# Second feed-forward layer: shift and scale made block by block at its beginning, 40 tiles of outer products with parts in SBUF

## Chip, cores and metric

One core of one Trainium2 chip runs the whole program. The metric is device time in microseconds (us), the median of three runs. A profile of one further execution comes with it; its trace is what is read here. PE is TensorE, DVE VectorE, ACT ScalarE, SP the engine whose queue issues nearly all DMAs.

## What is computed

A block of three sublayers on x (256 rows, width 2048), each scaled and shifted by numbers that come from a vector c:

```
mod = (silu(c) @ w_ada + b_ada).reshape(1, 3, 3, 2048)        # w_ada: 2048 x 18432
def sublayer(x, fn, pre, post, shift, scale, gate, weight):
    h = rms_norm(x, pre) * (1 + scale) + shift
    return x + weight * (1 + gate) * rms_norm(fn(h), post)
x = sublayer(x, ffn1, ..., mod[0,0], mod[0,1], mod[0,2], 0.5)
x = sublayer(x, mixer, ..., mod[1,0], mod[1,1], mod[1,2], 1.0)
x = sublayer(x, ffn2, ..., mod[2,0], mod[2,1], mod[2,2], 0.5)
# ffn(h) = (silu(h @ w_gate) * (h @ w_up)) @ w_down, inner width 5632
```

The mixer is a recurrent time mix (heads of 64) with a small pooling branch between two matrix products. All weights are float32 in device memory and pass through the chip once, 497.8 MB in all.

## The kernel before

**Products.** Each float32 weight piece is loaded by SP (`load`, L169, tile `raw`), split into a rounded part by ACT (L179, `hi`) and the rest by DVE (L180, `lo`), and multiplied in three terms. `mm3` (L189 to L191) issues three matmuls of 256 columns for one tile of 128 output columns and one of the 16 k-tiles of the input; `mm3_wide` (L196, L197) issues the same three terms as one matmul of 512 columns and one of 256. The input `hT` is held transposed, 16 k-tiles, each as rounded part and rest.

**Feed-forward layers.** `ffn` begins with `outer`: the k-tiles of `hT` come in blocks of 2, 2, 4, 4 and 4 (`FIRST_BLOCKS`, which `BLOCKS` equals), and each block is multiplied, as it becomes ready, into a number of gate and up tiles whose sums stay open. `first` of the 44 inner tiles keep their sums in PSUM; `spill` more have them in SBUF, where ACT copies the first part (L604) and DVE adds each later one (L606); their first two blocks are merged into one of four k-tiles (`MERGE`). The remaining inner tiles use `mm3_wide` over all 16 k-tiles. The inner tiles are taken in groups; after each group its down product is added to `y`. The first layer has `first` 4, `spill` 16 and groups of 20, 16, 8; the second has 6, 0 and groups of 12, 12, 12, 8.

**Next block.** Before a block of the second layer is multiplied, DVE updates x (L517), ACT scales its rows (L338), PE transposes them (L353), and ACT and DVE apply scale and shift (L357, L361, L362) with the columns in `mod`.

**Shift, scale, gate ("ada").** `ada_begin` lays down a list of tasks, `ada_step` takes the next quarter of one. A task is 1024 columns of `w_ada` over all 2048 rows (8 MB): SP loads 512 KB pieces into four (in the mixer two) buffers, DVE multiplies each by a column of silu(c) and adds it to `acc` (L242 the first, L244 the other 15), and at the end the 128 partitions are summed: for one vector by a DVE transpose and reduction (L256, L258) and matmuls L261; for a pair of vectors (shift and scale) by matmuls with ones, L251. The order is (1, 0) by blocks, then 2, 4, 3, 5, 7, 6, 8; vectors 7 and 6 are scale and shift of the second layer, 8 its gate. Steps are spread by counting loads: one per 2.8 loads in the first layer, one per 3 in the mixer, one per 12 in the second layer; in the outer product of the first layer, three per block (`TICKS`). `ada_finish` takes what is still missing at a place that needs it. The first layer gets through vectors 0 to 4 and 6 of the 8 steps of 5; 18 steps are left to the mixer (2 of vector 5, 8 each of 7 and 6), all taken by the end of its second `w_out` pass.

**Order.** A tile framework places the instructions of each engine from priorities; each engine then takes its own in order. `later` (L277) keeps ada work of DVE behind the first block's `hT` where a layer begins.

Of the kernel before, what the change touches and what calls it, by code (L numbers as in the profile page):

```python
# [23 lines left out]
FF_OUTER = 4  # L24
FF_SPILL = 16
MERGE = 4
FIRST_BLOCKS = ((0, 2), (2, 2), (4, 4), (8, 4), (12, 4))
TICKS = (1, 3, 7)
GROUPS1 = (20, 16, 8)
GROUPS2 = (12, 12, 12, 8)  # L30
ADA_FFN1, ADA_MIXER, ADA_OUT, ADA_FFN2 = 2.8, 3, 3, 12
BLOCKS = ((0, 2), (2, 2), (4, 4), (8, 4), (12, 4))
POOL_WIDTH = 512
# [43 lines left out]
class Block:  # L77
# [232 lines left out]
    def row(self):  # L310
        return self.tile(self.small, [P, 1], tag="row", bufs=32)
# [215 lines left out]
    def rows_block(self, load, nkt, per, x, banks, apart, done, more=(), warm=None, wide=1):  # L527
# [33 lines left out]
        for b, part in enumerate(parts):  # L561
# [4 lines left out]
            with self.tc.high_priority() if apart else nullcontext():  # L566
                done(*part, banks[b][:, :part[2]])

    def outer(self, blocks, loads, block, tick, piece):


# [3 lines left out]
        for q, (b0, bn) in enumerate(blocks):  # L575
            block(b0, bn)
            for i, (w, c0, n, outs, parts) in enumerate(loads):
                k0, kn = b0, bn
                if parts is not None and b0 + bn <= MERGE:
                    if b0 + bn < MERGE:  # L580
                        tick(q, i)
                        continue
                    k0, kn = 0, MERGE
                raw = self.load(w, k0, kn, c0, n)
                tick(q, i)
                nk = min(kn, (512 if self.gates else piece) // n)
                row, t0, t1 = outs, 0, KD - 1
                if parts is not None:
                    banks = [outs() for _ in parts]
                    row = [((2 * b + j) * P, bank[:, j, :], j == 0, j == 1) for b, bank in enumerate(banks)  # L590
                           for j in range(2)]
                    t0, t1 = k0, k0 + kn - 1
                for pc in range(0, kn, nk):
                    hi, lo = self.split(raw[:, pc:pc + nk, :])
                    for off, ps, first, last in row:
                        for k in range(nk):
                            kt = k0 + pc + k
                            cs = slice(off, off + P)
                            self.mm3(ps, hi[:, k, cs], lo[:, k, cs], self.hT[:, kt],
                                     first and kt == t0, last and kt == t1)  # L600
                if parts is not None:
                    for part, bank in zip(parts, banks):
                        if k0 == 0:
                            nc.scalar.copy(part, bank)  # L604
                        else:
                            nc.vector.tensor_tensor(part, part, bank, ALU.add)  # L606
# [141 lines left out]

    def tick(self):
        self.chunks += 1  # L750
        if int(self.chunks / self.every) > int((self.chunks - 1) / self.every) and self.ada_pos < self.ada_end[(6,)]:
            self.ada_step(self.mm)

    def mixer(self, ctx):
        nc, tc, I = self.nc, self.tc, self.I
# [37 lines left out]
        def stage(n, extra=None):  # L793
            runs = [extra] if extra else []
            if n - 1 in state:
                runs.insert(0, self.rwkv_m(n - 1, state[n - 1]))
            if n - 2 in state:
                runs.insert(0, self.rwkv_b(n - 2, state[n - 2]))
            while runs:
                runs = [run for run in runs if next(run, self) is not self]  # L800
# [43 lines left out]
        for q, tags in ((0, ("mm", "mm", "sa", "ga")), (2, ("pb", "zb")), (3, ("sb", "y", "mm"))):  # L844
            banks = [row(t) for t in tags]
            if q == 3:
                self.ada_finish((6,), self.mm)
            w = 2 if q == 0 else 1

            def load(kc):  # L850
                raw = self.load(I["w_out"], 4 // w * kc, 4 // w, q * 512, w * 512)
                self.tick()
                return raw

            def done(tt, c0, n, ps):
                self.post_rows(q + c0 // 512, tt, c0 % 512, n, ps)

            place = lambda tags: lambda shape: [self.tile(self.w2p, shape, F32R, tag=t, bufs=3 if t == "ar" else 2) for t in tags]
            more = [place(t) for t in (("SV", "S0"), ("ar", "bk")) * 2]
            self.rows_block(load, KD, 1, lambda k: self.hT[:, k], banks, q == 3, done, more, self.mm, w)  # L860
# [288 lines left out]
    def begin(self, mm):  # L1149

        nc, I = self.nc, self.I
        self.x = self.tile(self.big, [P, 2, D], tag="x")
        self.y = self.tile(self.big, [P, 2, D], tag="y")
        self.yT = self.y.rearrange("p t (k c) -> p (t k) c", c=T)
        self.hT = self.tile(self.big, [P, KD, 2, T], F32R, tag="hT")
        self.col = {}
        vec = lambda *names: [(n, I[n]) for n in names]
        self.csilu = self.tile(self.const, [P, KD], tag="csilu")
        nc.scalar.activation(self.csilu[:, :1], self.eps, AF.Silu)
        self.load_columns(vec("c"), mm)  # L1160
        for a, n, ap in self.columns("c", 0, KD):
            self.use_ln_exp([nc.scalar.activation(self.csilu[:, a:a + n], ap, AF.Silu)])
        self.ada_begin(((1, 0), (2,), (4,), (3,), (5,), (7,), (6,), (8,)))
        for i in range(5):
            if i == 3:
                for tt in range(2):
                    self.load_x(tt)
            if i == 1:
                self.load_columns(vec("norm_pre", "norm_post", "pool_scale", "k_k"), mm)
                self.load_columns([("b_ada", I["b_ada"][:P * P])], mm)  # L1170
            if i < 4:
                self.ada_step(mm)
        for tt in range(2):
            self.pre_begin(tt)
# [27 lines left out]
    def run(self):  # L1202
        I = self.I
        self.constants()
        with ExitStack() as ph:
            mm, actp = self.ffn_pools(ph)
            self.begin(mm)

            def block(k0, n):
                q = [b[0] for b in FIRST_BLOCKS].index(k0)  # L1210
                self.ada_finish(((1, 0), q), mm)
                for tt in range(2):
                    self.pre_rows(tt, k0, n)
                self.pre_block(0, k0, n, mm)

            def tick(q, i):
                if q == len(FIRST_BLOCKS) - 1:
                    if i == 0:
                        self.begin_rest(mm)
                elif i in TICKS:  # L1220
                    self.ada_step(mm)

            self.ffn(I["ffn1_w_gate"], I["ffn1_w_up"], I["ffn1_w_down"], ADA_FFN1, mm, actp, FIRST_BLOCKS, block, tick,
                     FF_OUTER, FF_SPILL, (FF_SPILL + FF_OUTER) // 2 - 8, GROUPS1,
                     lambda *a: (self.ada_finish((3,), mm), self.post_begin(0, 0.5, True, mm, *a)), lambda tt: None, True)
        with ExitStack() as ph:
            self.phase(ph, 2, 0, 2, 300)
            self.mixer(ph)
        with ExitStack() as ph:
            mm, actp = self.ffn_pools(ph)  # L1230

            def block(k0, n):
                self.next_block(2, k0, n, mm)

            self.ffn(I["ffn2_w_gate"], I["ffn2_w_up"], I["ffn2_w_down"], ADA_FFN2, mm, actp, BLOCKS,
                     block, lambda q, i: None, 6, 0, 0, GROUPS2,
                     lambda *a: (self.ada_finish((8,), mm), self.post_begin(2, 0.5, False, mm, *a)),
                     self.store, False)

# [26 lines left out]
```

## Time and profile before

| | us |
|---|---|
| median of three runs (2156.7 to 2158.58) | 2158.49 |
| the profiled execution's own time | 2157.36 |
| its span, first to last instruction | 2155.6 |
| PE busy | 2072.4 (96%) |
| DVE busy | 1621.2 (75%) |
| ACT busy | 1079.1 (50%) |

The span falls into the first layer (to about 805 us), the mixer (to about 1402) and the second layer. Read the share of an engine stage by stage, since the averages cover all three. The end of a pipelined matmul is modelled, so a PE that is shown as busy may still lose some time; how fast PE works is read from the starts of matmuls that follow each other. The mean granted clock was 0.984.

### The profile page before, as it was taken

The numbers are of one execution on the slowest core, as the hardware profiler recorded it, in microseconds if no ns is written. First come the engines' busy times: TensorE is split into PE (matmuls) and PEld (weight loads), VectorE is DVE, ScalarE is ACT, GpSimd is POOL, SyncE is SP. The second block draws the span as 40 slices with busy tenths as digits, with TensorE's granted clock in tenths as the row PEclk, the third lists the DMA queues.
The fourth block names the chain that finished last, engine by engine and source line by source line (L and its number), as shares of the span: only waits on it lengthen the run. The fifth ranks groups of instructions, "written<-read, shape, count | busy, mean of one in ns | idle before, by whom it ended". The sixth has DMA issues, their size and how long they took to land.

```text
span 2155.6 us, 37182 instructions
## 1 busy us (share of the span) xinstructions
PE 2072.4 (96%) x14955; PEld 1802.4 (84%) x14955; DVE 1621.2 (75%) x2523; ACT 1079.1 (50%) x1823; POOL 0.2 (0%) x4
## 2 busy tenths in 40 slices
PE   4999999999999998899999999999999999999998
PEld 3999988888888877888887866799888888888887
DVE  6788898798877778899998877788755555555556
ACT  4534543444433455765656654665434444444453
POOL 0000000000000000000000000000000000000000
PEclk8999999999999999999999979999999999999999
DMA  9999888999888748845644526599755555555553
GB/s 317 359 315 322 289 282 306 323 336 315 304 308 294 277 141 243 258 140 173 192 137 147 182 81 195 169 311 320 254 195 194 180 193 196 187 185 195 194 181 133
DMA packets 316570, 502.31 MB, mean 233 GB/s; under 512 B 12037, under 2 KB 197486, under 8 KB 316142
## 3 DMA queue, kind: packets, MB, share of 16 engines
q1 hardware_dynamic: 314380, 496.32, 68.6%
q10 hardware_dynamic: 2018, 3.62, 0.5%
q8 instruction: 117, 1.92, 0.4%
q14 instruction: 55, 0.45, 0.1%
HBM read 497.77 MB, written 2.12 MB: 232 GB/s over the span
## 4 chain that ended last, share of the span: by engine, by line
PE 83%; DMA 7%; DVE 6%; ACT 3%; issue 2%; SPq 0%; DVEq 0%; ACTq 0%
PE mm L196 21%; PE mm L197 10%; PE mm L191 7%; PE mm L190 7%; PE mm L189 7%; PE mm L523 7%; PE mm L525 7%; PE mm L524 7%; DMA ada<-in_w_ada_dram 5%; DVE lo L180 2%; DVE acc L244 1%; DMA raw<-in_w_in_dram 1%; ACT hi L179 1%; PE sb L1110 1%; PE sb L1145 0%
## 5 line engine op out<-in xcount | busy, mean ns | idle before, releaser
L179 ACT CAST hi<-raw 128x1024 fp32r<-128x1024 f32 (+2 forms) x768 | 694.6, 911 | 780.7 <-PE mm L525 266.9
L180 DVE TENSOR_TENSOR lo<-raw,hi 128x1024 fp32r<-128x1024 f32 (+2 forms) x768 | 796.4, 1048 | 351.6 <-ACT hi L179 348.5
L196 PE MATMUL mm<-hT,hi 128*128 128x512 f32 x1984 | 698.6, 395 | 0.0
L197 PE MATMUL mm<-hT,lo 128*128 128x256 f32 x1984 | 558.3, 281 | 2.4 <-DVE lo L180 2.4
L196 PEld LDWEIGHTS mm<-hT,hi 128*128 128x128 f32 x1984 | 373.8, 188 | 87.9
L244 DVE SCALAR_TENSOR_TENSOR acc<-ada,csilu,acc 128x1024 f32<-128x1024 f32 (+1 forms) x285 | 349.0, 1225 | 96.7 <-DMA ada<-in_w_ada_dram 94.7
L190 PE MATMUL mm<-hT,hi 128*128 128x256 f32 x1376 | 395.0, 288 | 3.4 <-DVE hT L362 3.4
L189 PE MATMUL mm<-hT,hi 128*128 128x256 f32 x1376 | 392.0, 289 | 4.0 <-ACT hT L357 3.8
L191 PE MATMUL mm<-hT,lo 128*128 128x256 f32 x1376 | 393.2, 287 | 0.5 <-DVE lo L180 0.5
L197 PEld LDWEIGHTS mm<-hT,lo 128*128 128x128 f32 x1984 | 372.8, 188 | 3.3 <-DVE lo L180 3.1
L189 PEld LDWEIGHTS mm<-hT,hi 128*128 128x128 f32 x1376 | 260.9, 191 | 10.6 <-ACT hT L357 6.1
L190 PEld LDWEIGHTS mm<-hT,hi 128*128 128x128 f32 x1376 | 261.9, 190 | 9.1 <-DVE hT L362 5.5
L191 PEld LDWEIGHTS mm<-hT,lo 128*128 128x128 f32 x1376 | 261.9, 191 | 4.5 <-DVE lo L180 0.7
L523 PE MATMUL mm<-hi,act 128*128 128x512 f32 (+1 forms) x688 | 264.9, 385 | 0.0
L524 PE MATMUL mm<-lo,act 128*128 128x512 f32 (+1 forms) x688 | 264.5, 384 | 0.0
L525 PE MATMUL mm<-hi,act 128*128 128x512 f32 (+1 forms) x688 | 264.4, 384 | 0.0
L524 PEld LDWEIGHTS mm<-lo,act 128*128 128x128 f32 x688 | 129.3, 188 | 25.9 <-DVE lo L180 0.6
L525 PEld LDWEIGHTS mm<-hi,act 128*128 128x128 f32 x688 | 129.3, 188 | 25.7
L523 PEld LDWEIGHTS mm<-hi,act 128*128 128x128 f32 x688 | 129.3, 188 | 25.6
L641 ACT ACTIVATE silu<-silu 128x512 f32<-128x512 f32 x31 | 19.6, 632 | 58.0 <-DVE silu L640 58.0
L644 ACT CAST act<-silu 128x512 fp32r<-128x512 f32 x31 | 19.2, 618 | 31.1 <-DVE silu L642 31.1
L606 DVE TENSOR_TENSOR act<-act,mm 128x512 f32<-128x512 f32 x48 | 32.2, 681 | 1.8 <-PE mm L191 1.6
(371 smaller groups left out, 1936.2 us busy)
## 6 DMA issues: line engine op xcount, KB each, us to landing
ada<-in_w_ada_dram SPq DMA_DIRECT2D x224, 512.0 KB
raw<-in_ffn_w_down_dram SPq DMA_DIRECT2D x88, 1024.0 KB
raw<-in_ffn_w_gate_dram SPq DMA_DIRECT2D x84, 1024.0 KB
raw<-in_ffn_w_up_dram SPq DMA_DIRECT2D x84, 1024.0 KB
raw<-in_w_in_dram SPq DMA_DIRECT2D x34, 1024.0 KB
ada<-in_w_ada_dram SPq DMA_DIRECT2D x128, 256.0 KB
raw<-in_w_out_dram SPq DMA_DIRECT2D x16, 1024.0 KB
raw<-in_w_in_dram SPq DMA_DIRECT2D x9, 512.0 KB
```

The lines of the kernel that those rows point to most:

```text
L179: a = nc.scalar.copy(hi, raw)
L180: d = nc.vector.tensor_tensor(lo, raw, hi.bitcast(F32), ALU.subtract)
L189: nc.tensor.matmul(ps, hi, x[:, 0, :], start=start, stop=False)
L190: nc.tensor.matmul(ps, hi, x[:, 1, :], start=False, stop=False)
L191: nc.tensor.matmul(ps, lo, x[:, 0, :], start=False, stop=stop)
L196: nc.tensor.matmul(ps.rearrange("p a t -> p (a t)"), hi, x.rearrange("p a t -> p (a t)"), start=start, stop=False)
L197: nc.tensor.matmul(ps[:, 0, :], lo, x[:, 0, :], start=False, stop=stop)
L244: self.later(nc.vector.scalar_tensor_tensor(acc, raw[:, i], ck, acc, ALU.mult, ALU.add))
L523: nc.tensor.matmul(ps, x[:, 0, ts], hi, start=start, stop=False)
L524: nc.tensor.matmul(ps, x[:, 0, ts], lo, start=False, stop=False)
L525: nc.tensor.matmul(ps, x[:, 1, ts], hi, start=False, stop=stop)
L606: nc.vector.tensor_tensor(part, part, bank, ALU.add)
```

## The change

The pair (7, 6) becomes five tasks by blocks, as (1, 0) is: 256, 256, 512, 512 and 512 columns of each vector. The mixer takes the first two (`ADA_AHEAD`); the other three, 24 MB in pieces of two 256 KB transfers, are taken in the second layer's outer product, three steps per block, and what is missing at the block that needs it. The second layer gets `first` 4, `spill` 16 (20 inner tiles, 40 of gate and up) and groups 20, 16, 8.

```diff
-GROUPS1 = (20, 16, 8)
-GROUPS2 = (12, 12, 12, 8)
+GROUPS = (20, 16, 8)
+ADA_AHEAD = 1
...
     def tick(self):
         self.chunks += 1
-        if int(self.chunks / self.every) > int((self.chunks - 1) / self.every) and self.ada_pos < self.ada_end[(6,)]:
+        if int(self.chunks / self.every) > int((self.chunks - 1) / self.every) and self.ada_pos < self.ada_end[(7, 6), ADA_AHEAD]:
...
             if q == 3:
-                self.ada_finish((6,), self.mm)
+                self.ada_finish(((7, 6), ADA_AHEAD), self.mm)
...
-        self.ada_begin(((1, 0), (2,), (4,), (3,), (5,), (7,), (6,), (8,)))
+        self.ada_begin(((1, 0), (2,), (4,), (3,), (5,), (7, 6), (8,)))
...
             def block(k0, n):
+                self.ada_finish(((7, 6), [b[0] for b in FIRST_BLOCKS].index(k0)), mm)
                 self.next_block(2, k0, n, mm)
-            self.ffn(I["ffn2_w_gate"], I["ffn2_w_up"], I["ffn2_w_down"], ADA_FFN2, mm, actp, BLOCKS,
-                     block, lambda q, i: None, 6, 0, 0, GROUPS2,
+            def tick(q, i):
+                if i in TICKS and self.ada_pos < self.ada_end[(7, 6)]:
+                    self.ada_step(mm)
+
+            self.ffn(I["ffn2_w_gate"], I["ffn2_w_up"], I["ffn2_w_down"], ADA_FFN2, mm, actp, FIRST_BLOCKS,
+                     block, tick, FF_OUTER, FF_SPILL, (FF_SPILL + FF_OUTER) // 2 - 8, GROUPS,
```

How this moves instructions is seen at three places. Names are the program's tiles with a running number: `lo` and `hi` the split weights, `x`, `hT` and `work` the next block's rows, `acc` and `ada` the sums and pieces of w_ada.

DVE where the second layer begins, from the last `hT` of its first block on. Before:

```order
L362 TENSOR_TENSOR hT_94<-work_15953,hT_94 128x256
L180 TENSOR_TENSOR lo_16002<-raw_15999,hi_16001 128x512
L180 TENSOR_TENSOR lo_16018<-raw_15999,hi_16017 128x512
L180 TENSOR_TENSOR lo_16036<-raw_16033,hi_16035 128x512
L517 SCALAR_TENSOR_TENSOR x_92<-y_93,row_15800,x_92 128x256
L180 TENSOR_TENSOR lo_16054<-raw_16051,hi_16053 128x512
L517 SCALAR_TENSOR_TENSOR x_92<-y_93,row_15892,x_92 128x256
```

and in the changed kernel:

```order
L362 TENSOR_TENSOR hT_94<-work_15815,hT_94 128x256
L180 TENSOR_TENSOR lo_15881<-raw_15861,hi_15880 128x512
L242 TENSOR_SCALAR acc_15863<-ada_15864,csilu_95 128x1024
L180 TENSOR_TENSOR lo_15897<-raw_15861,hi_15896 128x512
L244 SCALAR_TENSOR_TENSOR acc_15863<-ada_15868,csilu_95,acc_15863 128x1024
L517 SCALAR_TENSOR_TENSOR x_92<-y_93,row_15656,x_92 128x256
L244 SCALAR_TENSOR_TENSOR acc_15863<-ada_15872,csilu_95,acc_15863 128x1024
L517 SCALAR_TENSOR_TENSOR x_92<-y_93,row_15748,x_92 128x256
L244 SCALAR_TENSOR_TENSOR acc_15863<-ada_15876,csilu_95,acc_15863 128x1024
L180 TENSOR_TENSOR lo_15965<-raw_15962,hi_15964 128x1024
L244 SCALAR_TENSOR_TENSOR acc_15863<-ada_15912,csilu_95,acc_15863 128x1024
L362 TENSOR_TENSOR hT_94<-work_15950,hT_94 128x256
```

The products with the pieces of w_ada for the third block now stand between the updates and splits of the second. From the first row here (left out) to the sixteenth product DVE has 32 instructions, the 11 above among them: the 16 products, 2 splits of 512 columns and 4 of 1024, 2 updates of 256 and 6 of 512, and 2 `hT`.

SP's queue at the same place in the changed kernel, from the last load for the first block to the last for the second (before, pieces of w_ada stand there too, but nothing of this block waits for them):

```order
L169 DMA raw_15861<-in_ffn_w_up_dram 128x2x512
L238 DMA ada_15864<-in_w_ada_dram 128x512 x2
L238 DMA ada_15868<-in_w_ada_dram 128x512 x2
L238 DMA ada_15872<-in_w_ada_dram 128x512 x2
L238 DMA ada_15876<-in_w_ada_dram 128x512 x2
L169 DMA raw_15962<-in_ffn_w_gate_dram 128x2x512
L238 DMA ada_15912<-in_w_ada_dram 128x512 x2
L238 DMA ada_15916<-in_w_ada_dram 128x512 x2
L238 DMA ada_15920<-in_w_ada_dram 128x512 x2
L238 DMA ada_15924<-in_w_ada_dram 128x512 x2
L169 DMA raw_15992<-in_ffn_w_up_dram 128x2x512
```

The second block's weights now stand behind eight pieces, of which the last four wait for DVE to give back a buffer.

PE at the end of the second block's products with the four tiles whose sums stay in PSUM. Before (PE is at its products with the first block):

```order
L190 MATMUL mm_15950<-hT_94,hi_16053 128x256
L191 MATMUL mm_15950<-hT_94,lo_16054 128x256
L353 MATMUL mm_16076<-consts_69,y_93 128x128 x4
L353 MATMUL mm_16190<-consts_69,y_93 128x128 x4
L189 MATMUL mm_15945<-hT_94,hi_16089 128x256
```

and in the changed kernel:

```order
L190 MATMUL mm_15804<-hT_94,hi_16021 128x256
L191 MATMUL mm_15804<-hT_94,lo_16022 128x256
L251 MATMUL mm_16010<-ones_71,acc_15863 128x1 x8
L189 MATMUL mm_16051<-hT_94,hi_16053 128x256
L190 MATMUL mm_16051<-hT_94,hi_16053 128x256
```

The sum over partitions of the third block's shift and scale, L251, now stands in PE's row between the first 32 products of the layer (4 tiles of gate and of up, 4 k-tiles) and the 128 merged ones of the tiles with parts in SBUF. Before, no ada matmul stands in the outer product, and 48 products of the first two blocks are followed by those of the third.

## Rows read from the trace of the kernel before

**Rows 1.** Windows of the mixer and second layer: start:end, length, busy us by engine, clock.
```profile
860.00:1270.00 410.00, 391.59 (x4994) 338.53 (x4992) 365.35 (x945) 261.02 (x676) 0.00 (x0) 0.98 0.55 169
1270.00:1330.00 60.00, 54.45 (x427) 36.34 (x428) 42.69 (x101) 24.76 (x68) 0.00 (x0) 0.77 0.47 150
...
1560.00:1700.00 140.00, 140.00 (x733) 120.02 (x733) 75.80 (x79) 61.42 (x72) 0.00 (x0) 1.00 0.58 191
```

**Rows 2.** Chain that ended last, mixer: start, length, last matmul of a head pair.
```profile
961.87 0.86 PE sb L1145 x4
...
1026.57 0.87 PE sb L1145 x4
...
1237.77 0.86 PE sb L1145 x4
```

**Rows 3.** Timeline of PE, end of the mixer: start, length, instruction, [idle before, releaser].
```profile
1299.32 1.22 PE L882 MATMUL sa<-G,pool_w 128*128 128x256 f32 x2 [3.35 <-DVE G L880]
```

**Rows 4.** Timeline of PE, second layer, wide products: the first and the 29th.
```profile
1489.81 0.39 PE L196 MATMUL mm<-hT,hi 128*128 128x512 f32 x1
...
1499.70 0.40 PE L196 MATMUL mm<-hT,hi 128*128 128x512 f32 x1
```

**Rows 5.** Timeline of PE, first layer, outer product: the first and the 16th.
```profile
240.06 0.28 PE L189 MATMUL mm<-hT,hi 128*128 128x256 f32 x1
...
245.36 0.28 PE L189 MATMUL mm<-hT,hi 128*128 128x256 f32 x1
```

**Rows 6.** Instructions on `acc`, 805 to 1330: count, ns least/median/most, start of first and last.
```profile
L244 DVE SCALAR_TENSOR_TENSOR acc<-ada,csilu,acc x68: 1266/1278/1286, 816.9 to 1322.7; 128x1024 f32<-128x1024 f32 x68
```

**Rows 7.** Groups by line and shape, whole span: count, busy us, mean ns.
```profile
L244 DVE SCALAR_TENSOR_TENSOR acc<-ada,csilu,acc 128x512 f32<-128x512 f32 x30 | 22.5, 751 | 2.8 <-DMA ada<-in_w_ada_dram 2.0
```

**Rows 8.** Timeline of DVE where the second layer begins.
```profile
1403.64 0.42 DVE L362 TENSOR_TENSOR hT<-work,hT 128x256 fp32r<-128x256 f32 x1
1403.98 1.89 DVE L180 TENSOR_TENSOR lo<-raw,hi 128x512 fp32r<-128x512 f32 x3
1405.79 0.48 DVE L517 SCALAR_TENSOR_TENSOR x<-y,row,x 128x256 f32<-128x256 f32 x1
...
1413.80 0.74 DVE L517 SCALAR_TENSOR_TENSOR x<-y,row,x 128x512 f32<-128x512 f32 x1
1414.46 0.42 DVE L362 TENSOR_TENSOR hT<-work,hT 128x256 fp32r<-128x256 f32 x1
1414.80 0.74 DVE L517 SCALAR_TENSOR_TENSOR x<-y,row,x 128x512 f32<-128x512 f32 x1
...
1417.80 0.75 DVE L242 TENSOR_SCALAR acc<-ada,csilu 128x1024 f32<-128x1024 f32 x1
...
1427.72 1.28 DVE L244 SCALAR_TENSOR_TENSOR acc<-ada,csilu,acc 128x1024 f32<-128x1024 f32 x1
1428.92 1.22 DVE L180 TENSOR_TENSOR lo<-raw,hi 128x1024 fp32r<-128x1024 f32 x1
1430.05 1.28 DVE L244 SCALAR_TENSOR_TENSOR acc<-ada,csilu,acc 128x1024 f32<-128x1024 f32 x1
```

**Rows 9.** Timeline of SP: the first load issued for the second layer.
```profile
1394.13 0.37 SPq L169 DMA_DIRECT2D raw<-in_ffn_w_gate_dram  x1
```

**Rows 10.** DMA from 40 to 110, first layer: packets, bytes, mean rate.
```profile
DMA packets 13118, 25.05 MB, mean 358 GB/s; under 512 B 915, under 2 KB 925, under 8 KB 13112
```

**Rows 11.** Timeline of PE, outer product of the first layer.
```profile
42.55 1.87 PE L251 MATMUL mm<-ones,acc 128*128 128x1 f32 x8 [6.18 <-DVE acc L244]
...
101.54 1.84 PE L251 MATMUL mm<-ones,acc 128*128 128x1 f32 x16
...
283.87 0.40 PE L523 MATMUL mm<-hi,work 128*128 128x512 f32 x1
```

**Rows 12.** Window after the wait at 42.55; columns as in rows 1.
```profile
43.00:53.00 10.00, 9.12 (x42) 8.42 (x43) 7.73 (x11) 4.43 (x7) 0.00 (x0) 0.52 1.05 391
```

**Rows 13.** Timeline of PE, second layer: the first wide product.
```profile
1480.62 0.40 PE L196 MATMUL mm<-hT,hi 128*128 128x512 f32 x1
```

More of the change, by code (lines that the diff above doesn't have):

```diff
@@ L1223, in run @@
             self.ffn(I["ffn1_w_gate"], I["ffn1_w_up"], I["ffn1_w_down"], ADA_FFN1, mm, actp, FIRST_BLOCKS, block, tick,
-                     FF_OUTER, FF_SPILL, (FF_SPILL + FF_OUTER) // 2 - 8, GROUPS1,
+                     FF_OUTER, FF_SPILL, (FF_SPILL + FF_OUTER) // 2 - 8, GROUPS,
                      lambda *a: (self.ada_finish((3,), mm), self.post_begin(0, 0.5, True, mm, *a)), lambda tt: None, True)
```

## The prediction, made before the changed kernel ran

> **What bounds the kernel now.** I read the busy shares by windows first, then the chain that ended last, then the timelines where stages meet. In the second layer PE has no gap (140 us busy of 140), with DVE at 76 of 140. In the mixer both are nearly full: of 410 us PE is busy 391.6 and DVE 365.4. At the mixer's end, 1270 to 1330, PE is busy 54.5 of 60 at a mean granted clock of 0.77 [rows 1]. So work on DVE or in the DMA queues costs nothing in the second layer once it runs. In the mixer, less work on DVE can help, but only as far as PE is waiting there.
>
> How far, two views tell. In the chain the last matmul of a head pair's stage returns after 64.7 us the first time (961.87 to 1026.57), and in the next three periods after 70.4 on average (211.2 by 3) [rows 2]. One period has the same six loads and the same two ada steps as another, so 64.7 can be reached even with that load on DVE, and three periods lose 17 us to it. And at 1299.32 PE has stood 3.35 us, waiting for a small DVE instruction of the pooling [rows 3].
>
> **The change, part by part.**
>
> *Products.* 14 inner tiles, 28 of gate and up, go from `mm3_wide` to `mm3`: 448 products of one tile with one k-tile. A wide product takes 9.89 us by 28 = 0.353 us from start to start [rows 4], three narrow matmuls 5.30 by 15 = 0.353 [rows 5]. I take nothing for it. The Trainium skill speaks against the change here: "TensorE: Matmul & The Clock Gate", section "Wait — 56ns, not 53.3ns?", states a fixed cost of about 2.5 ns for each matmul at full clock. By that the 448 further matmuls would cost 1.1 us, an estimate; the rows show no such difference, and the measurement decides.
>
> *Sums in SBUF.* 16 copies on ACT and 48 additions on DVE are new, 8 additions to `y` (one group less) go. They lie beside PE's matmuls, as in the first layer, whose same loads I use below, so that their cost is in those rows. If that cover went, PE would wait at the end of the outer product; in the first layer it does not: the first down matmul follows without idle time [rows 11].
>
> *The mixer.* It had 18 ada steps of four products: 72 on DVE, 68 of them L244 at 1.28 us [rows 6]; the other 4 are the L242 that begin a task. It keeps 2 such steps (8 products) and gets 8 of half width: 32 products of 0.75 us [rows 7]. As one instruction starts some 0.08 us before the one ahead of it has ended (1.20 from start to start for 1.28) [rows 8], that is 85 us before and 9.6 + 32 x 0.67 = 31 us now: 54 us less on DVE, of 408 between 860 and 1330 [rows 1]. 32 MB less pass through SP's queue ahead of the mixer's weights, and 8 MB come back in halves, 24 MB less in all. What PE gains lies between nothing and all that it loses: 410 - 391.6 = 18.4 us, 60 - 54.5 = 5.5, and half of the 27.6 us that a mean clock of 0.77 means at the half level (60 x 0.23 = 13.8 lost) [rows 1]: 37.7. A loss I exclude: nothing is added there but ten or so tiny matmuls. I take half, 19 us; the slow periods and the wait above, 17 + 3.35 = 20, say about the same.
>
> *The beginning of the second layer.* Here is the new wait. L251 of the third block stands in PE's row behind the first 32 products, and needs all 16 DVE products of its task. DVE takes these in order, after the first block's `hT`, among the work of the second block. I add up the starts [rows 8]: 2 splits of 512 at 0.60 (1.81 by 3) = 1.2; 4 of 1024 at 1.13 = 4.5; the L242 0.75; 15 L244 at 1.20 = 18.0; 2 updates of 256 at 0.48 = 1.0; 6 of 512 at 0.66 = 4.0; 2 `hT` at 0.34 = 0.7. Together 30.1 us from 1403.98, so 1434.1 on the clock of before (all of this moves with the mixer's end). PE's own 32 products take 11.3 us; with the wait for the second block's rows they end at about 1418, an estimate, and PE stands some 16 us.
>
> Do the pieces arrive in time? SP begins at 1394.13 [rows 9]. 8 MB of w_ada and 3 MB of weights (0.5 four times, 1 once) at the 358 GB/s of the first layer's beginning [rows 10], which has transfers of the same size, take 31 us: 1425 or, with a buffer's turn of some us, a little more. DVE is later, and I take nothing; up to 6 us stay in the range. The rule of the skill against this: "DMA: Bandwidth & Descriptors", section "Bandwidth", asks for transfers of 1 MiB or more for three quarters of the peak, with 341 GB/s measured at 1 MB and 138 at 64 KB; these are of 256 KB. By it 8 MB at some 230 GB/s, an estimate between the two figures, would bring the last piece at 1440; the row's rate says 1425.
>
> Then, from 1434.1: L251 1.8 [rows 11]; the second block's other 128 products 128 x 0.353 = 45.2; and a low clock. After the 6.2 us wait at 42.55 the granted clock was 0.52 (1.2 GHz, nearly all the time) for the next 10 us, which costs 4.8 [rows 12]; I take the same. 1485.9. The last three blocks I take from the first layer, where L251 of the third block to the first down matmul takes 182.3 us with three such sums [rows 11]; here two are left, 180.5. 1666.4. Before, the outer product ended at 1480.6 [rows 13], and the 448 wide products that follow take 158.3: 1638.9 for the same work. **The second layer is 27.5 us longer.** Without the low clock it would be 22.7.
>
> *The end.* 84 counted loads at one step per 12 give 7 of vector 8's 8 steps; the last is taken at the final group, and PE now transposes the gate (L388) right before the last down products, waiting for a few DVE instructions. Nothing taken; at most a wait as in [rows 3], 3.4 us. With the 6 us above the upper end of the loss is 36.9.
>
> **Sum.** The profiled execution had a span of 2155.6 us and took 2157.36, which is 1.1 below the median of 2158.49. +27.5 - 19 = +8.5, so 2167 against the median.
>
> **Rivals.** A difference under 0.2%, some 4.3 us, can hardly be told from none.
>
> *The mixer gives back more.* DVE at 89% stands before PE in more places than idle time shows, since ends of matmuls are modelled; with 54 us less it would no longer be late, and the clock at the end would stay up. If PE gets all 37.7 us: 2158.5 + 27.5 - 37.7 = 2148, faster. It decides from a gain of 32 us on. For it: the clock of 0.77, three slow periods. Against it: the quick period has the full load, and most of the low clock lies where a chain of small steps ends.
>
> *They cancel.* A gain of 23 to 32 us: about 2158.
>
> *The mixer gives nothing.* PE is 95% busy there and sets the pace; periods differ for other reasons. 2158.5 + 27.5 = 2186.
>
> *The small pieces come slowly.* If w_ada came at two thirds of the rate of [rows 10], DVE would wait and L251 come 6 us later: 2173. It is the rule on transfers above; the row speaks against it.
>
> That the change does not do what it says I leave out: the order shows the products gone from the mixer and L251 in the new place.
>
> **How the numbers follow.** The forecast (2163 to 2180 around 2167) has 0.42, the mixer giving back more 0.24, cancelling 0.15, nothing gained 0.14, slow pieces 0.05. Slower is the first, fourth and fifth: 0.61; the same 0.15; faster 0.24. With the bounds, 22.7 - 37.7 = -15 to +36.9 around the median, the range runs from 2145 to 2190; it leaves out the most favourable tenth and the case in which nothing is gained and all else is late.
>
> **What would show it.** Right: in the second layer's first 35 us one L251 with idle time of about 16 us before it, released by `acc` on DVE, and a granted clock near 0.5 after it; the 640 products of the outer product ending some 27 us later than the same work did, counted from the first one. In the mixer 40 ada products, and 15 to 25 us less from its first to its last matmul. Wrong: an L251 that waits under 5 us; a mixer whose length has not changed, or is over 30 us shorter; or products of 256 columns that follow each other more slowly than 0.118 us.

## Result and the profile after

The changed kernel takes 2166.94 us (median of 8 runs, 2161.28 to 2171.99) where the kernel before takes 2157.68 beside it: a ratio of 1.0041, with an interval of 1.0024 to 1.0058, so 5 to 13 us slower. The forecast was 2167.0. The profiled execution has a span of 2166.3 us (2155.6 before). By stages, read from the starts of matmuls:

| us | before | after | difference | forecast |
|---|---|---|---|---|
| start to the first L203 (end of the first layer) | 802.2 | 800.1 | -2.1 | 0 |
| mixer: first L203 to the second layer's first L189 | 599.4 | 579.8 | -19.6 | -19 |
| second layer: first L189 to the start of the last wide product | 700.6 | 731.5 | +30.9 | +27.5 |
| from there to the end | 53.5 | 54.9 | +1.4 | 0 to 3.4 |

The first layer is the same code in both: 2 us is well within what one execution differs from another there (796.2 to 802.2 over all profiles of this document). The borders of the other stages, in the timeline of PE (start, length, instruction), before:

```profile
802.16 4.02 PE L203 MATMUL mm<-consts,ones 128*128 128x512 f32 x9
...
1401.51 0.50 PE L189 MATMUL mm<-hT,hi 128*128 128x256 f32 x2 [0.66 <-ACT hT L357]
```

and after, with the first down matmul:

```profile
800.09 4.45 PE L203 MATMUL mm<-consts,ones 128*128 128x512 f32 x10
...
1379.87 0.50 PE L189 MATMUL mm<-hT,hi 128*128 128x256 f32 x2 [0.66 <-ACT hT L357]
...
1646.64 0.39 PE L523 MATMUL mm<-hi,work 128*128 128x512 f32 x1
```

The outer product with its 640 products now takes 266.8 us (1379.87 to 1646.64). Before, its 192 took 79.1 [rows 13].

**The mixer.** Windows of the same lengths as in [rows 1], set 2 us earlier as the stage is (start:end, length, busy us of PE, PEld, DVE, ACT, POOL, granted clock, DMA share, GB/s):

```profile
858.00:1268.00 410.00, 402.45 (x5214) 346.46 (x5214) 329.80 (x937) 265.83 (x695) 0.00 (x0) 0.98 0.41 119
1268.00:1328.00 60.00, 57.16 (x304) 42.02 (x299) 35.93 (x83) 28.97 (x66) 0.00 (x0) 0.97 0.43 140
```

PE's busy time rises from 391.6 to 402.5 of 410 while DVE's falls from 365 to 330, and at the end the clock of 0.77 has become 0.97. Such windows do not hold quite the same work in both kernels; over the whole mixer DVE's busy time falls from 504 to 450 us, the 54 that were forecast. The instructions on `acc` between 800 and 1330, which answer [rows 6], are the 40 that were counted:

```profile
L244 DVE SCALAR_TENSOR_TENSOR acc<-ada,csilu,acc x38: 741/747/1284, 814.8 to 1046.6; 128x512 f32<-128x512 f32 x30, 128x1024 f32<-128x1024 f32 x8
...
L242 DVE TENSOR_SCALAR acc<-ada,csilu x2: 480/484/489, 847.6 to 981.7; 128x512 f32<-128x512 f32 x2
```

**The beginning of the second layer.** The timeline of DVE, which answers [rows 8]:

```profile
1381.99 0.43 DVE L362 TENSOR_TENSOR hT<-work,hT 128x256 fp32r<-128x256 f32 x1
1382.34 0.69 DVE L180 TENSOR_TENSOR lo<-raw,hi 128x512 fp32r<-128x512 f32 x1
1382.94 0.74 DVE L242 TENSOR_SCALAR acc<-ada,csilu 128x1024 f32<-128x1024 f32 x1
...
1397.16 1.23 DVE L180 TENSOR_TENSOR lo<-raw,hi 128x1024 fp32r<-128x1024 f32 x1 [1.24 <-ACT hi L179]
...
1409.72 1.23 DVE L180 TENSOR_TENSOR lo<-raw,hi 128x1024 fp32r<-128x1024 f32 x1 [2.05 <-ACT hi L179]
...
1413.20 2.60 DVE L244 SCALAR_TENSOR_TENSOR acc<-ada,csilu,acc 128x1024 f32<-128x1024 f32 x2
```

and of PE:

```profile
1386.19 0.28 PE L191 MATMUL mm<-hT,lo 128*128 128x256 f32 x1
...
1400.70 0.28 PE L191 MATMUL mm<-hT,lo 128*128 128x256 f32 x1
1415.85 3.58 PE L251 MATMUL mm<-ones,acc 128*128 128x1 f32 x16 [14.88 <-DVE acc L244]
1419.29 0.56 PE L189 MATMUL mm<-hT,hi 128*128 128x256 f32 x1
...
1466.84 1.03 PE L353 MATMUL mm<-consts,y 128*128 128x128 f32 x8
```

PE starts the last matmul of its first 32 products at 1400.70 and then stands for 14.9 us, until the last of DVE's 16 products on `acc` is done. DVE is not always busy in that time: twice it waits for `hi`, because the weights come late. The timeline of ACT says so:

```profile
1396.08 1.04 ACT L179 CAST hi<-raw 128x1024 fp32r<-128x1024 f32 x1 [5.49 <-DMA raw<-in_ffn_w_up_dram]
...
1408.64 1.99 ACT L179 CAST hi<-raw 128x1024 fp32r<-128x1024 f32 x2 [2.07 <-DMA raw<-in_ffn_w_gate_dram]
```

Windows around the wait show the low clock (columns as above):

```profile
1390.00:1400.00 10.00, 7.62 (x39) 6.94 (x40) 8.76 (x10) 2.26 (x4) 0.00 (x0) 0.66 0.93 324
1400.00:1419.00 19.00, 4.12 (x24) 3.93 (x22) 13.71 (x14) 7.49 (x9) 0.00 (x0) 0.60 0.94 328
1419.00:1425.00 6.00, 6.00 (x31) 6.00 (x32) 5.50 (x8) 0.00 (x0) 0.00 (x0) 0.56 0.99 360
1425.00:1485.00 60.00, 58.72 (x497) 58.28 (x496) 41.78 (x39) 33.87 (x45) 0.00 (x0) 1.00 0.87 301
```

**The end.** PE's L388 now waits for the gate, since vector 8 is finished too late:

```profile
2112.94 0.27 PE L388 MATMUL mm<-consts,gpost 128*16 128x128 f32 x1 [0.86 <-DVE gpost L386]
```

### The profile page after: what moved, and what is told of

Same layout as the page of the kernel before. It is cut to its first block, busy times and chain, and to the rows that moved or that the text cites. A ratio compares the mean times of both kernels' runs of the same rounds, so it can differ in the third digit from the quotient of the medians.

```text
span 2166.3 us, 38214 instructions
## 1 busy us (share of the span) xinstructions
PE 2076.9 (96%) x15435; PEld 1828.5 (84%) x15435; DVE 1635.6 (76%) x2543; ACT 1078.5 (50%) x1809; POOL 0.2 (0%) x4
## 4 chain that ended last, share of the span: by engine, by line
PE 79%; DMA 9%; DVE 7%; ACT 3%; issue 2%; SPq 1%; DVEq 0%; ACTq 0%
PE mm L196 15%; PE mm L191 9%; PE mm L190 9%; PE mm L189 9%; PE mm L197 8%; DMA ada<-in_w_ada_dram 6%; PE mm L523 6%; PE mm L524 6%; PE mm L525 6%; DVE lo L180 3%; DVE acc L244 2%; DMA raw<-in_w_in_dram 1%; ACT hi L179 1%; DMA raw<-in_ffn_w_gate_dram 1%; PE mm L251 1%
## 5 line engine op out<-in xcount | busy, mean ns | idle before, releaser
L196 PE MATMUL mm<-hT,hi 128*128 128x512 f32 x1536 | 539.8, 395 | 0.0
L190 PE MATMUL mm<-hT,hi 128*128 128x256 f32 x1824 | 521.6, 287 | 5.4 <-DVE hT L362 5.4
L189 PE MATMUL mm<-hT,hi 128*128 128x256 f32 x1824 | 518.5, 287 | 7.2 <-ACT hT L357 5.6
L189 PEld LDWEIGHTS mm<-hT,hi 128*128 128x128 f32 x1824 | 347.1, 192 | 13.8 <-ACT hT L357 8.3
L190 PEld LDWEIGHTS mm<-hT,hi 128*128 128x128 f32 x1824 | 348.5, 191 | 10.8 <-DVE hT L362 7.5
L196 PEld LDWEIGHTS mm<-hT,hi 128*128 128x128 f32 x1536 | 288.8, 188 | 67.7
L524 PE MATMUL mm<-lo,act 128*128 128x512 f32 (+1 forms) x656 | 252.2, 384 | 0.4 <-DVE lo L180 0.4
L523 PE MATMUL mm<-hi,act 128*128 128x512 f32 (+1 forms) x656 | 252.4, 385 | 0.0
L525 PE MATMUL mm<-hi,act 128*128 128x512 f32 (+1 forms) x656 | 251.9, 384 | 0.0
L524 PEld LDWEIGHTS mm<-lo,act 128*128 128x128 f32 x656 | 123.3, 188 | 25.6 <-DVE lo L180 1.5
L523 PEld LDWEIGHTS mm<-hi,act 128*128 128x128 f32 x656 | 123.3, 188 | 24.5
L525 PEld LDWEIGHTS mm<-hi,act 128*128 128x128 f32 x656 | 123.3, 188 | 24.4
L606 DVE TENSOR_TENSOR act<-act,mm 128x512 f32<-128x512 f32 x96 | 64.2, 682 | 1.9 <-PE mm L191 1.6
L251 PE MATMUL mm<-ones,acc 128*128 128x1 f32 x128 | 18.6, 273 | 34.5 <-DVE acc L244 34.5
L251 PEld LDWEIGHTS mm<-ones,acc 128*128 128x128 f32 x128 | 18.3, 226 | 35.3 <-DVE acc L244 35.2
```

The lines of the kernel that those rows point to most:

```text
L189: nc.tensor.matmul(ps, hi, x[:, 0, :], start=start, stop=False)
L190: nc.tensor.matmul(ps, hi, x[:, 1, :], start=False, stop=False)
L196: nc.tensor.matmul(ps.rearrange("p a t -> p (a t)"), hi, x.rearrange("p a t -> p (a t)"), start=start, stop=False)
L523: nc.tensor.matmul(ps, x[:, 0, ts], hi, start=start, stop=False)
L524: nc.tensor.matmul(ps, x[:, 0, ts], lo, start=False, stop=False)
L525: nc.tensor.matmul(ps, x[:, 1, ts], hi, start=False, stop=stop)
```

## Experiments

"Outer" is from the second layer's first L189 to the matmul that follows its last product; "first part" and "end" split the mixer at the first matmul of the fifth head pair's L1145 [rows 2]; "half clock" is the time at a granted clock near 0.5 in outer. All but the time and the ratio come from one profiled execution.

| kernel | time | ratio to before (interval) | mixer: first part + end | outer | half clock |
|---|---|---|---|---|---|
| before | 2157.68 | | 435.4 + 163.9 | 79.1 | 3 |
| after | 2166.94 | 1.0041 (1.0024 to 1.0058) | 424.7 + 155.1 | 266.8 | 27 |
| late_sum | 2155.48 | 0.9992 (0.9974 to 1.0010) | 420.9 + 155.2 | 258.2 | 14 |
| shape_only | 2166.83 | 1.0053 (1.0030 to 1.0076) | 442.6 + 164.0 | 241.6 | 7 |
| ahead2 | 2172.66 | 1.0074 (1.0055 to 1.0094) | 422.2 + 156.7 | 272.3 | 34 |
| few_products | 2134.73 | one run | 421.6 + 155.8 | 81.2 | 3 |
| one_step | 2156.46 | 0.9997 (0.9981 to 1.0014) | 418.8 + 155.1 | 258.4 | 17 |
| no_step | 2150.04 | 0.9952 (0.9932 to 0.9973) | 423.9 + 155.0 | 249.7 | 10 |
| ahead2_late | 2154.96 | 0.9995 (0.9973 to 1.0017) | 425.6 + 156.7 | 248.6 | 10 |
| no_loads | 2148.74 | one run | 438.8 + 153.6 | 80.1 | 7 |
| later_fourth | 2142.57 | 0.9932 (0.9913 to 0.9951) | 424.9 + 155.1 | 243.8 | 0 |
| early_steps | 2172.64 | 1.0085 (1.0051 to 1.0119) | 462.9 + 156.1 | 81.0 | 7 |
| ada_only | 2191.46 | 1.0159 (1.0138 to 1.0180) | 421.0 + 155.1 | 140.9 | 65 |

The mixer of shape_only has the same instructions in the same order as that of before, and yet it is 7 us longer there, in the one profile of each; the five kernels that share the changed kernel's mixer with it lie between 574.0 and 580.0. Differences of under some 7 us between two mixers prove nothing here.

**The two halves of the change: shape_only and ada_only.**

```diff
 # shape_only, against the kernel before
-                     block, lambda q, i: None, 6, 0, 0, GROUPS2,
+                     block, lambda q, i: None, FF_OUTER, FF_SPILL, (FF_SPILL + FF_OUTER) // 2 - 8, GROUPS1,
 # ada_only, against the changed kernel
-                     block, tick, FF_OUTER, FF_SPILL, (FF_SPILL + FF_OUTER) // 2 - 8, GROUPS,
+                     block, tick, 6, 0, 0, (12, 12, 12, 8),
```

> The kernel before, with only the second layer's shape changed (4 tiles in PSUM, 16 in SBUF, groups of 20, 16, 8); the pair (7, 6) stays in the mixer as before. Theory A, the shape costs nothing and the loss is the wait for w_ada: mixer as before (from its first to its last L203, 597 +- 3 us), 640 products in 235 to 243 us, time 2153 to 2162. Rival C, the shape costs by itself (sums in SBUF, only 16 products to cover a block's rows): 640 products in 250 us or more, time 2168 or more.

> The changed kernel's ada by blocks, with the shape of the kernel before (6 tiles in PSUM, none in SBUF, groups of 12, 12, 12, 8). A block of four k-tiles is 48 products, 17 us of PE, while 8 MB of w_ada and 3 MB of weights for it take 31 us at 358 GB/s. Theory A (the 40 tiles are what covers w_ada): PE waits for each of the last three blocks, the 192 products take 115 to 135 us instead of 79; mixer 574 to 582 us; time 2170 to 2190. If w_ada were covered anyway: 85 to 95 us, time 2143 to 2153.

The shape alone leaves outer at 241.6 us, within what the shape-costs-nothing theory asked, but the time at 2166.83 is above its 2162 and just under the rival's 2168. The trace accounts for 6.7 us: against before, from the second layer's first L189 to the last wide product it is 5.3 us longer, the end 1.5. Of the 5.3, 4.2 lie in outer, where before the 79.1 and the 158.3 of the same products as wide ones make 237.4. The interval of the ratio, 6 to 16 us, leaves open whether the shape costs more than this; ahead of the second layer the code is unchanged. So the shape costs a little by itself; one wait that shows is for `hT`, whose DVE instruction stands behind products of vector 8 and sums of the tiles (timeline of PE, shape_only):

```profile
1533.42 0.58 PE L190 MATMUL mm<-hT,hi 128*128 128x256 f32 x1 [4.27 <-DVE hT L362]
```

The ada alone is a little worse than even the first of its theories asked: outer goes from 79.1 to 140.9, the time to 2191.46. In outer PE waits 24.9 us for the sums, in three waits (timeline of PE, ada_only), and 16.9 us, in five, for `hi` of weights that stand behind the pieces:

```profile
1410.23 3.38 PE L251 MATMUL mm<-ones,acc 128*128 128x1 f32 x16 [3.56 <-DVE acc L244]
...
1448.48 3.54 PE L251 MATMUL mm<-ones,acc 128*128 128x1 f32 x16 [9.53 <-DVE acc L244]
...
1488.77 3.54 PE L251 MATMUL mm<-ones,acc 128*128 128x1 f32 x16 [11.84 <-DVE acc L244]
```

65 us of outer pass at half clock. Neither half is a gain; the 40 tiles are there to cover w_ada, and do so except at the beginning.

**Where the mixer's gain comes from: few_products, no_loads, early_steps.**

```diff
 # few_products, against the kernel before
+                elif v0 in (6, 7):
+                    self.later(nc.vector.scalar_tensor_tensor(acc[:, :, :16], raw[:, i, :, :16], ck, acc[:, :, :16], ALU.mult, ALU.add))
 # no_loads, against the kernel before
...
+            if v0 in (6, 7):
+                raw = self.consts[:, :width].unsqueeze(1).unsqueeze(1).broadcast_to([P, 1, 2, width])
...
 # early_steps, against the kernel before
-ADA_FFN1, ADA_MIXER, ADA_OUT, ADA_FFN2 = 2.8, 3, 3, 12
+ADA_FFN1, ADA_MIXER, ADA_OUT, ADA_FFN2 = 2.8, 2.2, 3, 12
```

> The kernel before, but of the 64 DVE products for vectors 7 and 6 the 60 of L244 take 32 of their 1024 columns (this part of shift and scale is left out); all loads of w_ada stay. Some 66 us less on DVE in the mixer. Theory E, the mixer gains from less work on DVE: from the first L189 after its beginning to the second layer's 18 to 28 us less than before, time 2130 to 2141. Rival F, it gains from fewer bytes ahead of its weights in SP's queue: 0 to 5 us less, time 2153 to 2159.

> The kernel before, but without the 32 MB of loads for vectors 7 and 6; all 64 products run in full on DVE, on constants (this shift and scale are left out). Theory E, DVE's work holds the mixer up: from its first L203 to the second layer's first L189 595 to 607 us (before 599.4, shape_only 606.6 with the same mixer), time 2152 to 2163. Rival F, the bytes ahead of the mixer's weights hold it up: 575 to 585 us, time 2132 to 2142.

> The kernel before, with one ada step per 2.2 loads instead of 3 in the mixer: the last nine products with vectors 7 and 6 come before the last head pairs instead of among the pooling and w_out. If the low clock and the waits at the mixer's end come from those products (no_loads, where they run early, has them 10 us shorter): from the fifth L1145 to the second layer 153 to 157 us (before 163.9, shape_only 164.0), the part ahead of it 0 to 8 us longer (before 429, shape_only 436), time 2148 to 2157. If the end is long for another reason: 163 us, time 2156 to 2165.

With the loads and hardly any products, the mixer is 577.4 us, as short as the changed kernel's. With the products and no loads it is 592.4, between both theories, as is the time, but the parts tell them apart: its first part (438.8) is that of the kernels with all products (435.4, 442.6), its end (153.6) that of the kernels with few. Without loads to wait for, DVE has taken all its products before the end begins (the last starts at 1238.1). early_steps pulls them forward with their loads: the end becomes 156.1 as its theory said, and the first part pays 20 to 28 us, not 0 to 8 (the 429 and 436 of its expectation are 435.4 and 442.6 as the table counts), so the kernel is slower than the one before. Its window (columns as above) shows PE 29 us short of 410, and a clock of 0.94:

```profile
860.00:1270.00 410.00, 381.03 (x4617) 326.25 (x4615) 353.40 (x885) 243.68 (x625) 0.00 (x0) 0.94 0.55 172
```

At the pace of before the loads cost nothing that shows: the first part of no_loads is as long as before's without a byte of w_ada for 7 and 6, and that of few_products, which has them all, is short. So the changed kernel's gain is DVE's, in both parts: some 9 us at the end, where products stood among the pooling, and some 17 in the first part (435.4 and 442.6 against 418.8 to 424.9). It is not in proportion. Between the start of the mixer and 1230, DVE spends on `acc` 35 us in the changed kernel and its kin (first part 419 to 425), 55 in ahead2 and ahead2_late (422, 426), 79.5 in before and shape_only (435, 443), and 91 in no_loads (439). The 463 of early_steps are another matter: its DVE spends 90 us there, no more than that of no_loads, so the 24 us between these two are not made by the number of products: early_steps has the loads at a closer pace, no_loads has none. Both have all 72 products in the first part; with the loads PE stands 32 us there instead of 20 and has 44 us at half clock instead of 20. Why, no run shows.

**Is it the place of L251? late_sum and ahead2.**

```diff
 # late_sum, against the changed kernel
-                if i in TICKS and self.ada_pos < self.ada_end[(7, 6)]:
+                if i in ((5, 7, 9) if q == 1 else TICKS) and self.ada_pos < self.ada_end[(7, 6)]:
 # ahead2, against the changed kernel
-ADA_AHEAD = 1
+ADA_AHEAD = 2
```

> The changed kernel, with the three ada steps of the second block's loads taken at loads 5, 7 and 9 instead of 1, 3 and 7, so that the third block's L251 stands 48 products (17 us) later in PE's row. Theory A, the place of L251 in PE's row makes PE stand: the 14.9 us wait goes, with some 2 us of L251 at half clock and 2.5 us of products at half clock after it; from the first L189 of the layer to the first down matmul 247 to 252 us instead of 266.8, time 2146 to 2152. Rival B, the beginning is bound by the transfers or by DVE and L251 only shows it: PE waits for hi and lo of the 128 merged products instead, 256 to 264 us, time 2157 to 2164.

> The changed kernel with the third block's task in the mixer as well. Theory A, the wait hangs on the place of the fourth ada step of the layer, whose L251 stands ahead of the merged products whichever block it is for: L251 (now the fourth block's) still waits 10 to 16 us, the second layer is as long as in the changed kernel, the mixer is 4 to 8 us longer by 16 more products on DVE; time 2170 to 2176. Rival D, the loss comes from the third block needing its task early: the wait goes, time 2150 to 2157.

ahead2 settles the first question. The third block's task is done in the mixer, nothing needs the fourth's until 100 us later, and PE stands all the same (timeline of PE, ahead2):

```profile
1413.03 3.57 PE L251 MATMUL mm<-ones,acc 128*128 128x1 f32 x16 [14.86 <-DVE acc L244]
```

It is the place of the layer's fourth step that makes the wait. That the mixer would pay 4 to 8 us for 16 more products was wrong (578.9); outer is 5.5 us longer instead, with 6.8 us more at half clock, from 1589 on. In late_sum the same instruction stands 48 products later and waits for nothing, but of the 19 us that its expectation adds up (14.9, 2 and 2.5) only 8.6 come back. Outer lands in the rival's range, the time between the two: PE now stands for the second block's `hT` and for the weights (timeline of PE, late_sum).

```profile
1388.21 0.58 PE L190 MATMUL mm<-hT,hi 128*128 128x256 f32 x1 [1.33 <-DVE hT L362]
1394.72 0.38 PE L189 MATMUL mm<-hT,hi 128*128 128x256 f32 x1 [1.40 <-ACT hi L179]
...
1403.24 0.58 PE L189 MATMUL mm<-hT,hi 128*128 128x256 f32 x1 [3.11 <-ACT hi L179]
...
1422.05 1.84 PE L251 MATMUL mm<-ones,acc 128*128 128x1 f32 x16
```

Both theories hold in part: L251's place costs PE about 9 us beyond what the beginning loses in any case; that the rest comes from the pieces of w_ada ahead of the weights, the next runs are to show.

**The pieces behind the weights: one_step, no_step, ahead2_late.** Each has a table of loads per block in place of `TICKS`:

```diff
-                if i in TICKS and self.ada_pos < self.ada_end[(7, 6)]:
+                if i in ((1,), (3, 5, 7, 9), (1, 3, 5, 7), (1, 3, 7), ())[q] and ...       # one_step
+                if i in ((), (3, 5, 7, 9), (1, 3, 5, 7), (1, 3, 5, 7), ())[q] and ...      # no_step
+                if i in ((), (3, 5, 7, 9), (1, 3, 5, 7), (), ())[q] and ...                # ahead2_late, ADA_AHEAD = 2
```

> The changed kernel, with one ada step (8 pieces) in the first block's loads, four in the second's (3, 5, 7, 9), four in the third's, three in the fourth's. Theory G, what is left of the loss in late_sum (some 15 us of waiting and half clock from 1380 to 1405) comes from the pieces of w_ada ahead of the second block's weights in SP's queue and from their products among the second block's rows on DVE: with 2 MB there instead of 6 MB the 640 products take 245 to 252 us (late_sum 258), time 2143 to 2150. Rival H, one step is enough to make the second block late, or L251 so late makes the third block wait: 255 to 262 us, time 2153 to 2160.

> The changed kernel, with no ada step in the first block's loads and four each in those of the second, third and fourth. Theory G: the second block has nothing of w_ada ahead of it, the 640 products take 240 to 246 us (241 in shape_only), the mixer stays as in the changed kernel, time 2138 to 2146. Rival H, the third block's L251 comes 4 steps of DVE work later, at the end of the second block's products, and PE waits there 8 us or more: 250 us or more, time 2148 or more.

> As no_step, but with the third block's task in the mixer and four ada steps each in the loads of the second and third block only. If the mixer takes 16 more products for nothing, as the profile of ahead2 shows (578.9 us against 579.8 and 576.1), and the beginning is free of w_ada: 640 products in 239 to 244 us, time 2137 to 2146, no worse than no_step. If the mixer pays for them at the rate of the 54 us that gave 20 (some 7 us for 20 us on DVE): 2145 to 2153.

With nothing of w_ada in the first block's loads (no_step) the beginning loses little, and the kernel is faster than the one before. The forecast of 240 to 246 for outer is missed by 4 us, by a wait that was not foreseen: PE comes to the fourth block's L251 before DVE has done its last product (timeline of PE, no_step), and 6.8 us of half clock follow. The time, 2150.0, lies in the rival's range, but the rival's wait did not come: the third block's L251 does not wait.

```profile
1484.36 2.93 PE L251 MATMUL mm<-ones,acc 128*128 128x1 f32 x16 [2.65 <-DVE acc L244]
```

one_step lands in its rival's ranges, and the rival holds in part: the third block's L251 makes PE wait as well (timeline of PE, one_step), and from the layer's first L189 to the third block's first L353 it takes 68.6 us against 61.9 in no_step. So a single step among the first block's loads costs some 7 us. The fourth block's L251 adds a wait of 3.6 us with 10.2 of half clock.

```profile
1423.10 1.92 PE L251 MATMUL mm<-ones,acc 128*128 128x1 f32 x16 [2.08 <-DVE acc L244]
```

The third block's task in the mixer (ahead2_late) brings nothing more: outer is 248.6, with a wait of 2.7 us at the same place as in no_step, the mixer is no shorter, and the time of 2155.0 misses both of its ranges. Why it is 5 us slower than no_step stays open.

**The last wait: later_fourth.**

```diff
-                if i in TICKS and self.ada_pos < self.ada_end[(7, 6)]:
+                if i in ((), (3, 5, 7, 9), (1, 3, 5, 9), (1, 3, 5, 7), ())[q] and ...
...
-ADA_FFN1, ADA_MIXER, ADA_OUT, ADA_FFN2 = 2.8, 3, 3, 12
+ADA_FFN1, ADA_MIXER, ADA_OUT, ADA_FFN2 = 2.8, 3, 3, 10
```

> As no_step, with the eighth ada step taken at load 9 of the third block instead of 7 (the fourth block's L251 stands later in PE's row), and the gate's steps one per 10 loads instead of 12, so that its last is not left for the final group. In no_step that L251 waits 2.65 us, is followed by 6.8 us of half clock, and the end from the last wide product is 54.9 us against 53.5 in the kernel before. If each of these is removed by its cause: 640 products in 241 to 246 us (no_step 249), the end 53 to 54 us, time 2140 to 2148 (no_step 2150). If the wait only moves (the third block's products are held by transfers): 249 us, time 2148 to 2152.

As the first theory had it. Outer is 243.8 us without any half clock, the end 53.8, and the kernel is 11 to 19 us faster than the one before. No L251 of the layer's beginning waits, nor does L388 (timeline of PE, later_fourth):

```profile
1434.50 1.92 PE L251 MATMUL mm<-ones,acc 128*128 128x1 f32 x16
...
1496.49 1.84 PE L251 MATMUL mm<-ones,acc 128*128 128x1 f32 x16
...
2090.09 0.27 PE L388 MATMUL mm<-consts,gpost 128*16 128x128 f32 x1
```

## Why the prediction was right

The time came out as forecast, and so did the mechanism: PE gets part of its lost time in the mixer back from DVE, and L251 stands in PE's row until DVE's products are done. That the time is met to a tenth of a us is luck. By the profiles, the loss behind the mixer was 32.3 us (30.9 and 1.4) for 27.5, and the gain in the mixer, over all of them, 25.5 for 19: errors of 5 and 6 us that cancel.

*Products: nothing.* Right. In the fourth block's products of the changed kernel, 101 products lie between these two starts (timeline of PE), 35.69 us or 0.353 each, against 0.353 for a wide one [rows 4]:

```profile
1600.71 0.28 PE L189 MATMUL mm<-hT,hi 128*128 128x256 f32 x1
...
1636.40 0.28 PE L189 MATMUL mm<-hT,hi 128*128 128x256 f32 x1
```

The fixed cost for each matmul in the Trainium skill's "TensorE: Matmul & The Clock Gate", section "Wait — 56ns, not 53.3ns?", does not show between 256 and 512 columns here.

*The mixer: 19 us, half of the 37.7 that it could give.* 19.6 in the pair of profiles. Over all profiles of the two mixers, it is 603.0 (two) against 577.5 (six: after, late_sum, one_step, no_step, later_fourth, ada_only), so 25.5: the half was a choice between two bounds, and rather too small. The reason given beside it, 17 us from three slow periods, did not come. In the changed kernel (chain that ended last) the four periods take 72.0 and then 66.4 on average, 271.2 together for 275.9 before [rows 2]:

```profile
953.64 0.86 PE sb L1145 x4
...
1025.61 0.86 PE sb L1145 x4
...
1224.88 1.06 PE sb L1145 x4
```

The last product on `acc` starts at 1046.6, and the last two periods, without any, still take 66.3 on average, where the quickest before took 64.7 with eight. Over all profiles some 10 us of the gain lie ahead of the first L1145, 7 in the four periods and 9 at the end. What the runs show is a DVE that holds PE up little when its products on `acc` take 35 or 55 us up to 1230 and more when they take 79.5, and nine products among the pooling at the end. That the clock at the end would rise was put with the rival; it did (0.77 to 0.97, and from 31 us of half clock to 3 in the end), but in place of the 19.3 us that idle time and clock could give there, 8.8 came. PE still loses 7.5 us of 410, where it lost 18.4 before [rows 1].

*The wait for L251.* DVE's 32 instructions were added up to 30.1 us. From 1382.34 to L251 at 1415.85 it took 33.5, of which 3.3 are the two waits for `hi`: the sum was right to a tenth of a us or two, and "DVE is later, and I take nothing" for the transfers was the step that was short, by 3.3 of the 6 us kept in the range. The rate was taken as 358 GB/s from [rows 10] and was 314 between 1380 and 1415 (the DMA view of the changed kernel):

```profile
DMA packets 5904, 11.00 MB, mean 314 GB/s; under 512 B 544, under 2 KB 544, under 8 KB 5902
```

(The 31 us also took 11 MiB for 11 MB; at 358 GB/s they are 32.2.) Both rates are of transfers of the same sizes, so these rows do not show that size made the difference. Between 1380 and 1416 SP's queue itself stood 15.6 us until DVE's products freed buffers of w_ada, while the DMA engines were 91% busy; which of the two made the weights late, no run separates. The rate of 230 GB/s, estimated in the prediction from two figures of the Trainium skill, "DMA: Bandwidth & Descriptors", section "Bandwidth", is further off than the first layer's row.

*PE stands some 16 us.* 14.9: L251 came 3.4 us late, and the last of the 32 products started at 1400.70, where the forecast's 1418 is 1396.4 on this clock (21.6 less), 4.3 late as well. The mechanism was right; ahead2 shows that the wait hangs on L251's place in PE's row, not on the block that needs it.

*L251, low clock, the last three blocks.* L251 took 3.4 us (1415.85 to 1419.29) and not 1.8, at half clock. Beside it the clock is low in the windows from 1390, ahead of the long wait (0.66, so at most 3.4 us lost of 10), and from 1419 (0.56, 2.6 of 6): at most 6 us, against the 4.8 that was taken behind the wait alone. From the layer's first L189 to the third block's first L353 it took 87.0 (forecast 84.4); from there to the first down matmul 179.8 (180.5).

*What the sum left out.* Up to the last wide product the layer became 30.9 us longer, not 27.5. Of the 3.4, 1.9 lie in outer (266.8 for 264.9), where the late weights are; 1.5 lie behind it, in the wide and down products: 464.8 us for 463.2 before. shape_only has 464.2 there, so most of it comes with the shape. At the end 1.4 were added, within the 0 to 3.4 named; taking a step per 10 loads gives 1.1 of it back.

*Rivals.* That the mixer gives nothing, or everything, is out: six profiles lie between 574 and 580, where before takes 599.4 and 606.6. The gain of 25.5 is within the 23 to 32 of "They cancel"; that rival's time did not come because the loss was larger than forecast too. "The small pieces come slowly" happened by half, 3.3 of its 6 us. None of the three signs named as wrong appeared.

## What to carry to other kernels

A small instruction that waits on another engine holds up whatever behind it in its engine's row could have run: here L251, under 2 us of work, stood 14.9 us, and 8.6 came back when it was placed 48 products later. Place it by when its operand will be ready, and put its loads behind those that the engine needs next. Here two edits of load numbers turned a change that lost 9 us into one that gains 15. Ask of an engine's load not what share it has on average but what part of the stage it stands in front of: of the 45 us of products taken off DVE in the mixer's first part, the first 25 gave nearly all, the last 20 nothing that the scatter lets show.

## What had not been expected of the hardware

Once PE stands, it pays again: after the 14.9 us the 16 matmuls of L251 took 3.58 us, against 1.84 where PE had been running (late_sum), and products followed at 0.64 us each until 1424, against 0.353. Over the profiles with 640 products, outer and its time at half clock go together: 0 to 10 us of it where outer is 242 to 250, 14 to 17 at 258, 27 at 266.8, 34 at 272.3. Cause and consequence are not told apart by these runs, but for one pair of profiles: later_fourth, which takes away the wait of 2.65 us at 1484, has none of the 6.8 us of half clock that follow it in no_step. And two profiles of the same mixer differ by 7 us (599.4, 606.6), with 41 and 55 us at half clock in them, the 14 more all in the first part; at half speed, an estimate, they would make 7 us, the whole difference. What starts it in one and not in the other stays open.
